# A delta-net inversion by squared 8x8 blocks, decays read as rows, and new cost estimates for the order of the work

## The chip, the core and the metric

The kernel runs on one core of one Trainium2 chip. The metric is the device time of one execution in microseconds (us), median of three runs. TensorE (PE in the profile; PEld is its loading of weights) multiplies matrices, VectorE (DVE) and ScalarE (ACT) do elementwise work, GpSimd (POOL) some more, SyncE (SP) issues most transfers.

## The reference, cut to what matters

One layer: modulated norm, one large input projection, two token mixers side by side (RWKV-7 time mixing and a chunked gated delta net, both in two directions, with 256 context tokens ahead of 256 latent tokens), a gated merge, an output projection, a SwiGLU feed-forward part, a last norm. The change lies in the delta net (8 heads of 128 channels):

```python
gc = jnp.cumsum(chunks(g), axis=-1)
diff = gc[..., :, None] - gc[..., None, :]
decay = jnp.where(incl, jnp.exp(jnp.where(incl, diff, 0.0)), 0.0)
lmat = jnp.where(strict, jnp.einsum('nbhik,nbhjk->nbhij', kb, kc) * decay, 0.0)
rhs = jnp.concatenate([vc * bc[..., None], kb * jnp.exp(gc)[..., None]], axis=-1)
sol = lax.linalg.triangular_solve(lmat, rhs, left_side=True, lower=True, unit_diagonal=True)
...
qk = jnp.where(incl, jnp.einsum('nbhik,nbhjk->nbhij', qc, kc) * decay, 0.0)
q_dec = qc * jnp.exp(gc)[..., None]
k_tail = kc * jnp.exp(gc[..., -1:] - gc)[..., None]
```

`triangular_solve` inverts I + lmat, a unit triangular matrix. The kernel works with chunks of 128 tokens, so with one 128x128 inverse per head, direction and chunk.

## The kernel before

**Stages.** First come the norm and the low-rank projections (`p0`). Then one woven stage holds both mixers and the input projection: the eight RWKV head pairs (`prepare`, `grams`, `inverse`, `values`, `scan`, about 140 to 845 us), then the eight delta-net heads (about 840 to 1385 us), with the weight products for both (`products`) and the rest of the modulation (`ada_rest`, GpSimd transfers and VectorE sums) as filler. After it come the merge products (`pa`, `pb`), `wout` and the feed-forward part.

**The order.** In the woven stage the order on TensorE, VectorE, ScalarE and GpSimd is fixed ahead of time by a planner (`Weave.run`). Each piece of work is a generator that yields operations, waits for PSUM banks (`pab`, two; `pib`, one; `psb`, two; `mmb`, three) or for named events ("gram", h). `Lane` gives each operation a cost, and the planner always takes the operation that can start earliest, then the lower rank. Its costs are never waited for on the chip, where engines wait on semaphores; they only set the order. A list of matmuls is issued in groups of 32; `LAT['turn']` is added where TensorE changes from one kind of product to another. Weights are split into two halves (`whi`, cast by ScalarE; `wlo`, the rest, by VectorE) and multiplied in three passes; the small products of the mixers are float32.

**A delta-net head h.** `features` makes k, v, q (convolution, SiLU, norm); `tokens` transposes k and v and scales k by the decays (`keg`, `kta`); `decays` makes the decay matrix `Ed` of both directions and the decayed queries `Qe`; `head_grams` makes the matrices `LT` and `PT`; `head_inverse` inverts; `head_scan` runs the four chunks with their state. `head_inverse` waits for ("gram", h) and for ("inv", h-1), `decays` for ("gram", h-1), `head_scan` for ("gscan", h-1).

**The inversion (`invert`).** The 128x128 matrix is two 64x64 blocks and their coupling; per head there are 16 blocks of 64 (nu=8 tiles, two halves h). The 16x16 diagonal blocks are inverted by substitution: the blocks are written to DRAM (`scr`), read back with one block per partition (`X`), solved in 15 steps of two VectorE operations, written to DRAM (`tscr`) and read back as `T0` and `Tx`. Then the blocks are doubled to 32 and 64 by small products with evictions between, and to 128 in `head_inverse`, which copies the result into `TF`. The RWKV pairs use the same function with nu=16.

**Decays.** `gm` is a triangular mask times the log decays; a product with `aft` gives the differences, ScalarE exponentiates, GpSimd masks; a product with `ones` gives the running sums for `Qe`.

Of the kernel before, what the change touches and what calls it, by code (L numbers as in the profile page):

```python
# [18 lines left out]
P = 128  # L19
# [10 lines left out]
LAT = dict(dma=2.4, v=1.0, s=1.0, hop=0.5, own=0.13, grp=32, crank=-1, cg=4, turn=0.09)  # L30
# [7 lines left out]
for _name, _w in (("ident", 128), ("ones", 128), ("bd64", 128), ("rmask", 256),  # L38
                  ("qmask", 64), ("tri", 256), ("aft", 256), ("q4", 4), ("q2", 2),
                  ("eps", 1), ("gneps", 1)):  # L40
    _C[_name] = (_n, _n + _w)
    _n += _w
# [12 lines left out]
def const_array():  # L55
# [15 lines left out]
    put("qmask", np.concatenate([(same & (rb % 2 == 1))[:, even], (same & (rb % 2 == 0))[:, ~even]], 1))  # L71
    u = i[:, None]
    v = i[None]
    put("tri", np.concatenate([u <= v, u >= v], 1))
    put("aft", np.concatenate([u > v, u < v], 1))
# [35 lines left out]
class Lane:  # L111
# [5 lines left out]
    def __getattr__(self, name):  # L117

        def op(out, *a, **k):
# [49 lines left out]
class Weave:  # L169
# [55 lines left out]
    def run(self):  # L225
        while self.work:
# [41 lines left out]
def emit(ctx: ExitStack, tc, A, out, dbg=None):  # L268
# [34 lines left out]
    qmask = c_("qmask").rearrange("p (d a c) -> p d a c", d=2, a=2)  # L303
    tri = c_("tri").rearrange("p (d t) -> p d t", d=2)
    aft = c_("aft").rearrange("p (d t) -> p d t", d=2)
# [23 lines left out]
    zero = cst.tile([P, 130], F32, name="zero")  # L329
    G.memset(zero, 0.0)  # L330
# [74 lines left out]
    with tc.tile_pool(name="p0", bufs=1) as p0, \  # L405
# [95 lines left out]
        for part in range(NE + 1):  # L501
# [16 lines left out]
            else:  # L518
                for _ in before:
                    pass  # L520
        for t in tscr:
# [30 lines left out]
    def invert(pool, Lt, parts, nu, which, full, fill):  # L552

# [42 lines left out]
        yield v.transpose(T0[:, us[1]], Tx[:, us[1]])  # L596

# [6 lines left out]

        def half(t, d):
            ax = "p u"[:2 * len(t.shape) - 3]
            return t.rearrange(f"{ax} (a b c) -> {ax} a b c", a=2, b=2)[..., d, :]

        def mm(ps, d, lhs, rhs):
            return [e.matmul(ps[64 * h:64 * h + 64, 32 * i:32 * i + 32], lhs(h, h2 * d + i), rhs(h, h2 * d + i),  # L610
                             start=True, stop=True) for i in range(h2) for h in range(2)]

        Qm = xt[:, :32 * nu].rearrange("p (u c) -> p u c", c=32)
        for d in range(2):
            T0d = half(T0[:, us[d]], d)
            ps = yield pib
            yield mm(ps, d, Lt, lambda h, u: half(N_(h, u), d))
            pv = ps[:, 0:32 * h2].rearrange("p (i a c) -> p i a c", a=2, c=16)
            yield v.tensor_mul(Qm[:, us[d]].rearrange("p i (a c) -> p i a c", a=2), pv,
                               qmask[:, d].unsqueeze(1).to_broadcast([P, h2, 2, 16]))  # L620
            yield mm(ps, d, Nt_, lambda h, u: Qm[64 * h:64 * h + 64, u, :])
            yield v.tensor_add(T0d, pv, T0d)
            weave.release(pib)
            yield v.transpose(Tx[:, us[d]], T0[:, us[d]])
# [19 lines left out]
        qo = pool.tile([P, h2, 32], F32, tag="ivo", name="qo")  # L644
# [6 lines left out]
        if full:  # L651
# [3 lines left out]
            for h in range(2):  # L655
# [8 lines left out]
    abd = dpool.tile([4, 32, P], F32, name="abd")  # L664
    gtok = cst.tile([P, 4, 16], F32, name="gtok")
# [12 lines left out]
               ("ivo", 256, 1), ("iv0", 1024, 1), ("v", 512, 1), ("gt", T, 1))  # L678
# [152 lines left out]
    def grams(p, d):  # L831
# [7 lines left out]
        def four(ops):  # L839
            for o in ops:  # L840
                o.cost *= 0.5
# [199 lines left out]
    def products():  # L1041
# [24 lines left out]
        while todo or nxt:  # L1066
# [27 lines left out]
            else:  # L1094
# [5 lines left out]
    gplaces = (("kvq", 1280, 2), ("l2s", 512, 1), ("gm", 512, 1), ("Ed0", 512, 1), ("Ed1", 512, 1), ("eq", T, 1), ("ob", 8 * T, 1),  # L1100
               ("NW", 1024, 1), ("O", T, 1), ("gy2", T, 1), ("q3", T, 1), ("XT", 512, 1), ("prod", 64, 1))
    shared = dict(kta=("LAl0", 1024, 3), LTg=("LAl1", 1024, 3), keg=("ivx", 1024, 2), iv0=("LAc0", 512, 3), ivx=("LAc0", 512, 3),
                  vt=("LAc1", 512, 3), PT0=("LAc1", 512, 3), PT1=("Pm", 512, 3), Qe=("Pm", 512, 3), Vn=("bon", T, 3), ivo=("bon", T, 3),
# [24 lines left out]
    gs = Shared()  # L1128
    hd = [{} for _ in range(NGH)]
# [6 lines left out]
    def begin():  # L1136
# [6 lines left out]
        t2 = gs.tile([P, 512], F32, tag="gm", name="t2")[:, 0:P]  # L1143
# [12 lines left out]
        for n in (15, 13, 11, 9, 7, 5, 3):  # L1156
# [5 lines left out]
        yield v.tensor_scalar(sp, sp, al, -1.0, ALU.mult, ALU.mult)  # L1162
        ps = yield pab
        yield [e.transpose(ps[:, 0:P], sp, ident), e.transpose(ps[:, P:2 * P], bet, ident)]
# [4 lines left out]
        yield [e.matmul(ps[:, T + 64 * i + 32 * d:T + 64 * i + 32 * d + 32], m[:, d], gtok[:, :, 8 * d:8 * d + 8], start=True, stop=True)  # L1169
               for d in range(2) for i, m in enumerate((tri, aft))] + [e.matmul(ps[:, 3 * P:3 * P + 64], ones, gtok, start=True, stop=True)]  # L1170
        for i, t in enumerate((egc, eta)):
            for d in range(2):
                o = T + 64 * i + 32 * d
                yield s.activation(t[:, :, 8 * d:8 * d + 8], ps[:, o:o + 32].rearrange("p (b c) -> p b c", b=4), AF.Exp)
        yield s.activation(egl, ps[:, 3 * P:3 * P + 64].rearrange("p (b c) -> p b c", b=4), AF.Exp)
# [38 lines left out]
    def features(h):  # L1214
# [5 lines left out]
        if h > 1:  # L1220
            for n in ("tok", "gram"):
# [12 lines left out]
    def tokens(h):  # L1234
# [24 lines left out]
    def decays(h):  # L1259
# [3 lines left out]
        if h:  # L1263
            yield "gram", h - 1
        o["Ed"] = Ed = []
        qe = []
        for d in range(2):
            col = 8 * d + h
            gm = gs.tile([P, 4, P], F32, tag="gm", name="gm")
            yield v.tensor_mul(gm, tri[:, d].unsqueeze(1).to_broadcast([P, 4, P]),  # L1270
                               gtok[:, :, col:col + 1].to_broadcast([P, 4, P]))
            gf = gm.rearrange("p b c -> p (b c)")
            ps = yield pab
            yield e.matmul(ps, aft[:, d], gf, start=True, stop=True)
            ed = gs.tile([P, 4, P], F32, tag=f"Ed{d}", name="Ed")
            yield s.activation(ed.rearrange("p b c -> p (b c)"), ps, AF.Exp)
            weave.release(pab)
            yield g.tensor_mul(ed, ed, tri[:, d].unsqueeze(1).to_broadcast([P, 4, P]))
            Ed.append(ed)
            if d == 0:  # L1280
                yield "feat", h
                yield "scan", NPAIR - 1 if h else NPAIR - 2
                if h > 1:
                    yield "gscan", h - 2
                o["Qe"] = gs.tile([P, 2, T], F32, tag="Qe", name="Qe")
            ps = yield pab
            yield e.matmul(ps[:, :T], ones, gf[:, 0:T], start=True, stop=True)
            eq = gs.tile([P, T], F32, tag="eq", name="eq")
# [410 lines left out]
```

## Time and profile before

| | us |
|---|---|
| median of 3 runs | 2342.38 |
| lowest, highest | 2339.14, 2345.67 |
| profiled execution | 2348.77 |
| its span, first to last instruction | 2346.7 |
| busy: PE, DVE, ACT, POOL | 2223.8, 1557.2, 1047.9, 113.5 |
| granted TensorE clock, mean | 0.975 |

A busy PE is not PE at its peak: matmuls are pipelined and their ends are modelled. L142 is the line of a helper that emits every planned operation, so groups are told apart by their tiles: `mm` are weight products, `pi` those of the inversions, `pa` and `s` other small products. Tiles cut from one large buffer are all named `arena` (`keg`, `kta`, `LT`, `Vn`, `TF`, `Tx`, `T` have names of their own). In a timeline the columns are start, duration, engine, line, operation, and tiles written and read; in a row of grouped lines, count, busy time, mean ns of one, and idle time before with what ended it.

### The profile page before, as it was taken

What the parts mean: (1) busy time and instruction counts of PE and PEld (TensorE: products, weight loads), DVE (VectorE), ACT (ScalarE), POOL (GpSimd) and SP (SyncE); (2) the same over time, 40 slices, a digit from 0 to 9 for tenths busy, and PEclk for the clock granted to TensorE, in tenths of its full rate; (3) what the DMA queues carried; (4) which work ended last, traced back from release to release, by engine and by line L of the source; (5) the groups of instructions that cost most, each with busy time, mean ns of one, the idle gap of its engine ahead of it and who ended that gap; (6) DMA issues with size and microseconds to landing.
All of it is one profiled execution on the core that took longest, in us unless ns stands there. A gap on an engine that the chain in (4) does not pass through costs nothing. (4 is left out here: it accounts for less than half of the span.)

```text
span 2346.7 us, 51488 instructions
## 1 busy us (share of the span) xinstructions
PE 2223.8 (95%) x21368; PEld 1951.7 (83%) x21368; DVE 1557.2 (66%) x3237; ACT 1047.9 (45%) x1863; POOL 113.5 (5%) x183
## 2 busy tenths in 40 slices
PE   7988999999999999999798999999999999999998
PEld 4767677778788777776677989999999999999997
DVE  3447588778986489889878645765666556545454
ACT  3246454544355544344234346544444444444443
POOL 0000000000000011111111003000000000000000
PEclk9999999999999999999789999999999999999999
DMA  9956454434344256657466565663777776566665
GB/s 377 397 148 189 152 134 102 111 83 117 100 109 133 85 172 207 189 167 217 145 191 194 182 219 180 209 214 107 239 233 234 234 238 218 187 185 194 191 191 165
DMA packets 232570, 430.58 MB, mean 183 GB/s; under 512 B 114832, under 2 KB 130064, under 8 KB 227984
## 3 DMA queue, kind: packets, MB, share of 16 engines
q1 hardware_dynamic: 204688, 351.78, 48.4%
q0 software_dynamic: 13824, 50.34, 7.0%
q10 hardware_dynamic: 13824, 25.17, 3.5%
q8 instruction: 167, 2.74, 0.5%
q14 instruction: 67, 0.55, 0.1%
HBM read 401.45 MB, written 25.77 MB: 182 GB/s over the span
## 5 line engine op out<-in xcount | busy, mean ns | idle before, releaser
L357 DVE TENSOR_TENSOR wlo<-wraw,whi 128x1024 fp32r<-128x1024 f32 x328 | 393.5, 1200 | 351.1 <-ACT whi L356 348.2
L356 ACT CAST whi<-wraw 128x1024 fp32r<-128x1024 f32 x328 | 337.7, 1030 | 472.8 <-PE mm L367 413.8
L142 PE MATMUL mm<-hxh,wlo 128*128 128x256 f32 (+1 forms) x1376 | 468.3, 340 | 9.9 <-DVE wlo L142 9.7
L142 PE MATMUL mm<-hxh,whi 128*128 128x256 f32 (+1 forms) x1376 | 469.0, 341 | 3.4 <-ACT whi L142 3.3
L142 PE MATMUL mm<-hxl,whi 128*128 128x256 f32 (+1 forms) x1376 | 468.3, 340 | 0.0
L368 PE MATMUL mm<-hfh,wlo 128*128 128x256 f32 x1344 | 377.1, 281 | 0.4 <-DVE wlo L357 0.4
L366 PE MATMUL mm<-hfh,whi 128*128 128x256 f32 x1344 | 376.5, 280 | 0.0
L367 PE MATMUL mm<-hfl,whi 128*128 128x256 f32 x1344 | 375.2, 279 | 0.0
L142 PEld LDWEIGHTS mm<-hxh,wlo 128*128 128x128 f32 x1376 | 265.6, 193 | 39.4 <-DVE wlo L142 13.0
L142 PEld LDWEIGHTS mm<-hxh,whi 128*128 128x128 f32 x1376 | 265.6, 193 | 31.5 <-issue 6.5
L142 PEld LDWEIGHTS mm<-hxl,whi 128*128 128x128 f32 x1376 | 265.8, 193 | 27.2 <-issue 6.1
L142 DVE TENSOR_TENSOR wlo<-wraw,whi 128x512 fp32r<-128x512 f32 x344 | 236.2, 690 | 62.7 <-ACT whi L142 60.0
L142 ACT CAST whi<-wraw 128x512 fp32r<-128x512 f32 x344 | 205.8, 618 | 112.1 <-PE mm L142 88.9
L366 PEld LDWEIGHTS mm<-hfh,whi 128*128 128x128 f32 x1344 | 253.4, 189 | 0.0
L368 PEld LDWEIGHTS mm<-hfh,wlo 128*128 128x128 f32 x1344 | 252.8, 188 | 0.6 <-DVE wlo L357 0.6
L367 PEld LDWEIGHTS mm<-hfl,whi 128*128 128x128 f32 x1344 | 253.2, 188 | 0.0
L142 DVE TENSOR_TENSOR arena<-arena 128x28 f32<-128x28 f32 (+13 forms) x538 | 132.0, 247 | 32.1 <-DMA arena<-scr 20.4
L366 PE MATMUL mm<-za,whi 128*128 128x256 f32 x512 | 141.8, 277 | 0.0
L367 PE MATMUL mm<-za,whi 128*128 128x256 f32 x512 | 141.7, 277 | 0.0
L368 PE MATMUL mm<-za,wlo 128*128 128x256 f32 x512 | 141.6, 277 | 0.0
L142 DVE SCALAR_TENSOR_TENSOR aw<-aw,ck 128x512 f32<-128x512 f32 x180 | 131.2, 739 | 5.1 <-DMA aw<-ada_rest 4.4
L368 PEld LDWEIGHTS mm<-za,wlo 128*128 128x128 f32 x512 | 96.2, 188 | 0.0
(311 smaller groups left out, 3924.5 us busy)
## 6 DMA issues: line engine op xcount, KB each, us to landing
wraw<-w SPq DMA_DIRECT2D x172, 512.0 KB, 4.3
wraw<-wgu SPq DMA_DIRECT2D x168, 512.0 KB, 4.5
aw<-ada_rest POOLq DMA_DIRECT2D x96, 512.0 KB, 4.7
aw<-ada_first SPq DMA_DIRECT2D x32, 1024.0 KB, 11.5
wraw<-wdn SPq DMA_DIRECT2D x64, 448.0 KB, 3.7
wraw<-wout SPq DMA_DIRECT2D x32, 512.0 KB, 4.7
aw<-ada_gt ACTq DMA_DIRECT2D x64, 256.0 KB, 5.0
wraw<-wdn SPq DMA_DIRECT2D x32, 512.0 KB, 3.6
```

Of the source, the lines that this page charges most:

```text
L142: return Op(self, cost, lambda: getattr(self.engine, name)(out, *a, **k), split)
L356: S.copy(hi[:, c, :M], raw[:, c, :M])
L357: V.tensor_sub(lo[:, c, :M], raw[:, c, :M], hi[:, c, :M].bitcast(F32))
L366: E.matmul(ps, hi, Xh[:, k, :n], start=first and i == 0, stop=False)
L367: E.matmul(ps, hi, Xl[:, k, :n], start=False, stop=False)
L368: E.matmul(ps, lo, Xh[:, k, :n], start=False, stop=last and i == len(wt) - 1)
```

## The change

It changes four things.

- **Inversion of the delta-net heads.** `by_rows` is the old substitution, which the RWKV pairs keep. The heads use `by_squares`: the 8x8 diagonal blocks N are cut out by a mask, and the inverse is (I+N)(I+N^2)(I+N^4), made by products of 64x64x64 in five sets of 16; `double(8)` then takes the blocks to 16. `double` handles both directions in one batch, for the pairs as well.
- **Decays from rows.** `begin` makes running sums with a scan, writes them to DRAM (`cumd`), and `decays` reads them back as rows broadcast to all partitions; the differences are a per-partition add and a minimum with 0 before the exponential. The products with `aft` and `ones` and the masks `gm` go. `Qe` is made in a part of its own, with an event ("Qe", h) that other pieces wait for.
- **Moves.** `keg`, `kta` and `Vn` are scaled by ScalarE instead of VectorE (sixteen operations of 128x128 for four of 128x512; eight for eight).
- **Planner.** New costs for small products and for a change of kind; buffers for `LT` are taken once and kept.

```diff
-LAT = dict(dma=2.4, v=1.0, s=1.0, hop=0.5, own=0.13, grp=32, crank=-1, cg=4, turn=0.09)
+LAT = dict(dma=2.4, v=1.0, s=1.0, hop=0.5, own=0.13, grp=32, crank=-1, cg=4, turn=0.15)
...
-                if rows < 64:
-                    cost = 0.024
-                elif rows == 64:
-                    cost = max(0.066, 0.027 + 0.0008 * n)
-                elif rows < P or m == P:
-                    cost = 0.0054 + 0.00167 * n
-                else:
-                    cost = 0.107
+                tiles = max(1, P // rows) * max(1, P // m) if rows < 96 or m < 96 else 1
+                if tiles > 1:
+                    split = rows, m
+                cost = max(0.033 if tiles < 16 else 0.012, (0.0054 + 0.00167 * n) / min(tiles, 3))
...
-                    start += LAT["turn"]
-                self.split = ops[0].split
+                    start += LAT["turn"] if isinstance(ops[0].split, tuple) or isinstance(self.split, tuple) else 0.02
+                self.split = ops[-1].split
...
+    def by_squares(pool, Lt, parts, nu):
+        a, b, c = (pool.tile([P, nu, 64], F32, tag=t, name=n) for t, n in (("XT", "Dt"), ("iv0", "Dn"), ("ivx", "B")))
...
+        for h in range(2):
+            yield v.tensor_mul(*(t.rearrange("p (d u) c -> p d u c", d=2) for t in (a[hs[h]], parts(h))),
+                               m8[hs[h]].to_broadcast([64, 2, nu // 2, 64]))
+        yield v.transpose(b, a)
+        p1 = yield pib
+        p2 = yield pab
+        yield mm(p1, a, b) + mm(p2, b, a)
+        for h in range(2):
+            yield v.tensor_add(c[hs[h]], b[hs[h]], ident[hs[h], hs[h]].unsqueeze(1).to_broadcast([64, nu, 64]))
+        yield s.copy(flat(E2[:, 0]), p1)
+        weave.release(pib)
+        yield v.tensor_copy(flat(E2[:, 1]), p2)
+        weave.release(pab)
+        p1 = yield pib
+        p2 = yield pab
+        yield mm(p1, E2[:, 1], c) + mm(p2, E2[:, 0], E2[:, 1])
+        yield v.tensor_add(flat(b), p1, flat(c))
+        weave.release(pib)
+        yield s.copy(flat(a), p2)
+        weave.release(pab)
+        p1 = yield pib
+        yield mm(p1, a, b)
+        yield v.tensor_add(flat(c), p1, flat(b))
+        weave.release(pib)
+        yield v.transpose(b, c)
+        yield from double(8, Lt, c, b, flat(a), nu)
+        return c, b, flat(a)
+
+    def double(n, Lt, T0, Tx, xt, nu):
...
+        yield mm(ps, Lt, lambda h, u, d: half(T0[64 * h:64 * h + 64, u, :], d))
+        for d in range(2):
+            yield v.tensor_mul(Qm[:, us[d]].rearrange("p i (a c) -> p i a c", a=na), pv[:, us[d]],
+                               qmask[n == 8][:, d].unsqueeze(1).to_broadcast([P, h2, na, n]))
+        yield mm(ps, lambda h, u: Tx[64 * h:64 * h + 64, u, :], lambda h, u, d: Qm[64 * h:64 * h + 64, u, :])
+        for d in range(2):
+            T0d = half(T0[:, us[d]], d)
+            yield v.tensor_add(T0d, pv[:, us[d]], T0d)
+        weave.release(pib)
+        yield v.transpose(Tx, T0)
...
         def four(ops):
             for o in ops:
-                o.cost *= 0.5
+                o.cost *= 1.0
...
+        yield v.tensor_tensor_scan(t0, ones, sp, 0.0, ALU.mult, ALU.add)
+        yield v.tensor_tensor_scan(t1[:, ::-1], ones, sp[:, ::-1], 0.0, ALU.mult, ALU.add)
+        for d, t in enumerate((t0, t1)):
+            dq(cumd[d], t)
...
-            yield v.tensor_mul(keg[:, d], p4, egc[:, :, col:col + 1].to_broadcast([P, 4, P]))
-            yield v.tensor_mul(kta[:, d], p4, eta[:, :, col:col + 1].to_broadcast([P, 4, P]))
+            for b in range(4):
+                yield s.activation(keg[:, d, b], p4[:, b], AF.Identity, scale=egc[:, b, col:col + 1])
+                yield s.activation(kta[:, d, b], p4[:, b], AF.Identity, scale=eta[:, b, col:col + 1])
...
-            gm = gs.tile([P, 4, P], F32, tag="gm", name="gm")
-            yield v.tensor_mul(gm, tri[:, d].unsqueeze(1).to_broadcast([P, 4, P]),
-                               gtok[:, :, col:col + 1].to_broadcast([P, 4, P]))
-            gf = gm.rearrange("p b c -> p (b c)")
-            ps = yield pab
-            yield e.matmul(ps, aft[:, d], gf, start=True, stop=True)
             ed = gs.tile([P, 4, P], F32, tag=f"Ed{d}", name="Ed")
-            yield s.activation(ed.rearrange("p b c -> p (b c)"), ps, AF.Exp)
-            weave.release(pab)
+            a = cumd[d][0:1]
+            yield dq(ed, bass.AP(a.tensor, a.offset + col * P, [[0, P], [32 * P, 4], [1, P]]))
+            eq = gs.tile([P, T], F32, tag=f"eq{d}", name="eq")
+            yield s.activation(eq, ed[:, 0:2].rearrange("p b c -> p (b c)"), AF.Exp)
+            for b in range(4):
+                yield v.tensor_scalar(ed[:, b], ed[:, b], gtok[:, b, col:col + 1], 0.0, ALU.add, ALU.min)
+            yield s.activation(ed, ed, AF.Exp)
             yield g.tensor_mul(ed, ed, tri[:, d].unsqueeze(1).to_broadcast([P, 4, P]))
...
-            yield e.matmul(ps[:, :T], ones, gf[:, 0:T], start=True, stop=True)
-            eq = gs.tile([P, T], F32, tag="eq", name="eq")
-            yield s.activation(eq, ps[:, :T], AF.Exp)
...
-                yield v.tensor_scalar_mul(Vn[:, d, :], ps[:, P * d:P * d + P], btok[:, bs[d], 8 * d + h:8 * d + h + 1])
+                yield s.activation(Vn[:, d, :], ps[:, P * d:P * d + P], AF.Identity, scale=btok[:, bs[d], 8 * d + h:8 * d + h + 1])
```

More of the change, by code (lines that the diff above doesn't have):

```diff
@@ L550, in unit_rows, with by_rows @@
         return bass.AP(a.tensor, a.offset + (2 * u0 + h) * UNIT, [[64, 64], [2 * UNIT, nu], [1, 64]])
-    def invert(pool, Lt, parts, nu, which, full, fill):
+    def by_rows(pool, parts, nu, which, fill):
         h2 = nu // 2
@@ L598, in N_, with invert @@
+    def invert(pool, Lt, parts, nu, which, full, fill):
+        h2 = nu // 2
+        us = (slice(0, h2), slice(h2, nu))
+        T0, Tx, xt = yield from (by_rows(pool, parts, nu, which, fill) if which is not None else by_squares(pool, Lt, parts, nu))
         def N_(h, u):
@@ L602, in Nt_ @@
             return Tx[64 * h:64 * h + 64, u, :]
[L605 to L624, printed above, removed]
+        yield from double(16, Lt, T0, Tx, xt, nu)
         quads = []
@@ L664, in emit @@
     abd = dpool.tile([4, 32, P], F32, name="abd")
+    cumd = [dpool.tile([P, P], F32, name=f"cumd{d}") for d in range(2)]
     gtok = cst.tile([P, 4, 16], F32, name="gtok")
@@ L1355, in head_scan @@
         yield "tok", h
+        yield "Qe", h
         if h:
```

101 lines of the change are left out of this document (68 added, 33 removed).

## The prediction

> **What bounds the kernel now.** I read the page first, then the time by stage, then when each head's inversion starts and ends, and last the waits of that stretch. The page says TensorE, 95% busy.
>
> ```profile
> span 2346.7 us, 51488 instructions
> PE 2223.8 (95%) x21368; PEld 1951.7 (83%) x21368; DVE 1557.2 (66%) x3237; ACT 1047.9 (45%) x1863; POOL 113.5 (5%) x183
> ```
>
> That is an average over stages, so the busy time by stretch comes next. 400 to 800 us is recurrent time mixing at its steadiest. 837 to 1385 us runs from the first head's inversion to the last head's scan; the two stretches inside it are the first head and the fifth. After 1385 us come only projections and the feed-forward part.
>
> ```profile
> core 0: us, PE busy (x) PEld busy (x) DVE busy (x) ACT busy (x) POOL busy (x), PEclk, DMA share, GB/s
> 400.00:800.00 400.00, 397.07 (x5220) 312.66 (x5220) 312.60 (x778) 194.93 (x483) 11.24 (x30) 1.00 0.40 107
> 837.00:901.00 64.00, 59.73 (x501) 50.02 (x500) 55.94 (x132) 30.06 (x57) 10.81 (x17) 1.00 0.70 214
> 1101.00:1178.00 77.00, 61.31 (x450) 47.77 (x449) 59.78 (x150) 29.59 (x49) 12.12 (x20) 0.81 0.55 166
> 837.00:1385.00 548.00, 497.06 (x4286) 418.61 (x4284) 443.67 (x1108) 225.73 (x427) 70.44 (x110) 0.94 0.62 187
> 1385.00:2347.00 962.00, 931.14 (x7882) 925.53 (x7882) 537.26 (x718) 430.57 (x563) 21.23 (x16) 0.99 0.65 204
> ```
>
> Three things are to be seen. From 400 to 800 us TensorE idles 3 us in 400 at full clock: that stage is bound by its work. In the head stage it idles 548 - 497 = 51 us, at a granted clock of 0.94. The 962 us after it are not touched by the change and are full. So only the head stage has time to give, and the question is what holds it. The first and last rows of the inversions, and the timeline around the fifth head (number 4), tell:
>
> ```profile
> L153 SPq DMA_DIRECT2D scr<-LT x16: 595/596/620, 837.1 to 1306.6; - x16
> ...
> L142 ACT COPY TF<-pi x16: 361/367/372, 897.3 to 1365.7; 64x256 f32<-64x256 f32 x16
> ```
>
> ```profile
> 1086.76 1.12 DVE L142 SCALAR_TENSOR_TENSOR LT<-pa,nbtok,arena 128x128 f32<-128x128 f32 x4
> ...
> 1100.19 0.76 ACT L142 COPY TF<-pi 64x256 f32<-64x256 f32 x2 [1.03 <-PE pi L142]
> ...
> 1102.65 0.42 DVE L142 STREAM_TRANSPOSE T<-LT 64x256 f32<-64x256 f32 x1
> ...
> 1107.38 0.59 SPq L153 DMA_DIRECT2D arena<-scr  x1
> ...
> 1133.93 0.58 SPq L153 DMA_DIRECT2D tscr<-arena  x1
> ...
> 1142.70 0.30 PE L142 MATMUL pi<-T,LT 64*64 64x32 f32 x2
> ...
> 1177.64 0.75 ACT L142 COPY TF<-pi 64x256 f32<-64x256 f32 x2
> ```
>
> Head 4's matrix is complete at 1087.9, but its inversion begins at 1102.7, right behind head 3's last copy at 1101.0: `head_inverse` waits for ("inv", h-1). The eight inversions stand end to end from 837.1 to 1366.0: 529 us, 66 each, all but the whole stage. Inside head 4's, 40 us pass (1102.7 to 1142.7) before the first product: to DRAM, back as rows, thirty small VectorE steps, to DRAM, back. VectorE stands still for two of these trips, 41 us in the stage:
>
> ```profile
> DVE Tx L142 <- DMA T<-tscr: 21.8, 7, 5.9
> ...
> DVE arena L142 <- DMA arena<-scr: 19.2, 7, 7.1
> ```
>
> **The change, part by part.** Per-head prices come from the grouped rows of the head stage (the full transpose's from the whole run):
>
> ```profile
> L142 DVE TENSOR_TENSOR arena<-arena 64x15 f32<-64x15 f32 (+8 forms) x247 | 49.0, 198 | 22.2 <-DMA arena<-scr 19.2
> ...
> L142 DVE TENSOR_SCALAR Vn<-s,btok 128x128 f32<-128x128 f32 x64 | 21.0, 338 | 3.5 <-PE s L142 3.4
> ...
> L142 DVE TENSOR_TENSOR keg<-pa,egc 128x512 f32<-128x512 f32 x14 | 9.5, 678 | 1.3 <-PE pa L142 1.3
> ...
> L142 DVE TENSOR_TENSOR arena<-C,gtok 128x512 f32<-128x512 f32 x14 | 9.4, 673 | 0.1
> ...
> L142 DVE STREAM_TRANSPOSE Tx<-T 128x256 f32<-128x256 f32 x24 | 10.5, 439 | 21.9 <-DMA T<-tscr 21.8
> ...
> L142 DVE STREAM_TRANSPOSE Tx<-arena 128x512 f32<-128x512 f32 x24 | 16.9, 704 | 21.0 <-DMA arena<-tscr 20.8
> ...
> L142 DVE TENSOR_TENSOR arena<-pi,C 128x128 f32<-128x128 f32 x16 | 4.6, 285 | 3.0 <-PE pi L142 2.9
> ...
> L142 ACT CAST whi<-wraw 128x512 fp32r<-128x512 f32 x154 | 91.6, 617 | 72.4 <-PE mm L142 67.3 <-DVE arena L142 2.1 <-DVE aw L142 1.6
> ...
> L142 ACT COPY arena<-s 128x128 f32<-128x128 f32 x16 | 3.6, 265 | 17.5 <-PE s L142 17.3
> ```
>
> *VectorE.* Removed: the substitution, 49.0/8 = 6.1; four 128x512 products for `keg` and `kta`, 2.7; two masks `gm`, 1.35; eight `Vn`, 2.7; four transposes of half size, 1.75. Sum 14.6 us. Added: two masks and two identity sums at 0.68 (the 128x512 row, the nearest), 2.7; one eviction and two sums of that size, 2.0; two full transposes at 0.70, 1.4; in `double(8)` four operations at 0.285 and a transpose, 1.85; eight `tensor_scalar` of 128x128 for the decays, bounded by 0.2 (the small SBUF steps) and 0.34 (`Vn`), taken at 0.285, 2.3. Sum 10.2 us; `double(16)` turns two half transposes into one full one, -0.2. Net -4.6 a head, -37 us in all; and the 41 us of standing still for DRAM go too.
>
> *ScalarE.* Sixteen scalings and eight `Vn` at 0.265, 6.4, and two evictions of 512 columns at 0.62 (the cast of that size): +7.6 a head, +61 us. That is 226 + 61 = 287 of some 530 us, hidden beside TensorE. Were the cover gone, the `whi` casts of the next weights queue behind these 24 operations, and TensorE waits.
>
> *The queues.* SP loses ten transfers a head (of some 0.6 us of issue, as the row of `scr<-LT` shows) and gains two, the decay rows for `Ed0` and `Ed1`. These wait until `head_grams` of the head before has read the buffer; behind them on SP stand the `wraw` loads, covered by three buffers. The rows' trip to DRAM in `begin` is hidden: `begin` copies its scalars at 747.8, and the first `LT` that needs the decays is written at 832.1.
>
> ```profile
> L142 DVE COPY gtok<-pa x1: 225/225/225, 747.8 to 747.8; 128x64 f32<-128x64 f32 x1
> ```
>
> ```profile
> L142 DVE SCALAR_TENSOR_TENSOR LT<-pa,nbtok,arena x64: 308/342/354, 832.1 to 1304.9; 128x128 f32<-128x128 f32 x64
> ```
>
> GpSimd keeps its two mask products a head. I cost these at nothing.
>
> *TensorE.* Added: 80 products of 64x64x64 (16+16, 16+16, 16) and 32 of 64x64x32 in `double(8)`. What such a batch costs among the weights:
>
> ```profile
> 1005.29 0.60 PE L142 MATMUL pa<-arena,C 128*128 128x256 f32 x2
> ...
> 1014.66 1.10 PE L142 MATMUL pa<-arena,C 128*128 128x512 f32 x2 [0.70 <-DVE arena L142]
> ...
> 1347.72 0.28 PE L142 MATMUL mm<-hxh,whi 128*128 128x256 f32 x1
> ...
> 1347.83 0.28 PE L142 MATMUL mm<-hxl,whi 128*128 128x256 f32 x1
> ...
> 1348.04 0.66 PE L142 MATMUL pi<-T,LT 64*64 64x32 f32 x16
> ...
> 1348.62 0.19 PEld L142 LDWEIGHTS mm<-hxh,wlo 128*128 128x128 f32 x1
> ...
> 1363.84 0.68 PE L142 MATMUL pi<-Tx,arena 64*64 64x64 f32 x16
> ```
>
> Sixteen records are eight products (each float32 product has two), and hold TensorE from 1348.04 to 1348.62, 0.58 us; the step into the batch is 0.21 where weights follow at 0.11, so changing kind costs 0.10. 64 columns take as long as 32 (0.68 against 0.66). Added: 14 x 0.58 + 5 x 0.10 = 8.6; two batches fewer in `double(16)`, -0.2. Removed: two float32 products of 512 columns and two of 256, 2 x 1.10 + 2 x 0.60 = 3.4, or 2.9 if a drain of 0.12 is taken from each. Net +5.5 a head, +44 us; the ends are 36 (3.4 removed, no kind changes) and 57 (0.68 a batch).
>
> [...]
>
> *Latency.* From its first product at 1142.7 to its end at 1178.4 head 4 has nine product batches, 4.0 us each with the evictions between. The new inversion replaces 40 us by three VectorE operations (2.1) and five batches (20), and `double(16)` loses two batches (-8): 26 us less, so some 40 instead of 66 a head, 320 us for eight. The chain then no longer fills the stage. What is late next is TensorE: 497 + 44 = 541 us of work.
>
> *The planner's numbers* (small products cheaper, 0.15 for a change of kind) move instructions, not their durations. In the time-mixing stage there are 3 us to win in 400. The 16 merged batches of `invert` save 16 x 0.10 = 2 us; beyond it, a reordering can be worth a per cent of that stage either way, which I take as 0 +- 7.
>
> **Sum.** Of 51 us idle I leave 8 (twice the rate of 400 to 800). A clock of 0.94 means that 0.06 x 548 = 33 us of full-speed time were not granted; with the long waits gone I take 20 of them back. 541 + 8 - 20 = 529 against 548, -19; with the 2 above -21, rounded -22. The profiled execution took 2348.8 us (span 2346.7) and comes to 2327; the median of the runs is 6.4 us lower, so 2342.4 - 22 = **2320**.
>
> [...]
>
> **The rivals.** *All of it comes back.* No idle but 4 us, the full clock, the low end of the added work: 497 + 36 + 4 - 33 = 504, 44 less, 2298. For it: 400 to 800 us does run so. Against: the heads' products wait on evictions far more often.
>
> *TensorE is already the bound.* The added 44 us land on a queue whose idle time comes from other waits (scans, evictions, ScalarE now fuller), so 51 us idle and 0.94 stay: 2342 + 44 - 2 = 2384, and 2363 if a quarter (21) of the 51 + 33 = 84 us of idle and lost clock is won. It decides the sign where less than half of these 84 (42) is won. For it: 497/8 = 62 us of work a head, and 5.5 more, make 67.6, about the head's whole period of 68.5. Against: the inversions stand end to end.
>
> *Nothing comes of it.* The shorter chain pays just for the added products, or the order loses elsewhere what it wins: 2342.
>
> **How the numbers follow.** The forecast 0.56, with its own range 2305 to 2338 (the products' bounds 36 and 57 alone give 2312 to 2333, 10 to 30 us of clock alone 2310 to 2330); all back 0.15; TensorE the bound 0.17; nothing 0.12. 0.3% is 7 us, about what a measurement of this kernel can tell. Faster: 0.56 and 0.15, less a hundredth: 0.70; same 0.12; slower 0.18. The range runs from 2296, the first rival, to 2360, short of the second one's milder case.
>
> **What would show it.** Right: inversions of about 40 us with gaps between them, no VectorE wait on DRAM trips for heads, TensorE busy some 520 us of a head stage of 529, at a clock near 0.98, VectorE about 37 us less, ScalarE about 60 more. Wrong: inversions still end to end, a stage clock still at 0.94, `whi` casts late behind the scalings, or a time-mixing stage that moves by over 7 us.

## The result, and the profile after

The changed kernel takes 2357.14 us (median of 4 runs, 2355.13 to 2360.75) against 2340.98 before: ratio 1.0068, 95% interval 1.0047 to 1.0088. It is 16 us slower; 2320 had been forecast, 22 us faster. The profiled execution took 2356.19 us. Every stretch shown here and below comes from one profiled execution, which can lie 10 us from the median of its kernel (before: 2348.77 against 2340.98), so a few us between two stretches mean little. First the page of the changed kernel, then its busy time by stretch (columns as before):

```profile
span 2354.4 us, 54837 instructions
PE 2247.9 (95%) x23090; PEld 1988.6 (84%) x23090; DVE 1540.0 (65%) x3001; ACT 1108.9 (47%) x2071; POOL 116.8 (5%) x183
```

```profile
400.00:800.00 400.00, 396.20 (x5185) 315.00 (x5184) 316.75 (x793) 197.37 (x485) 14.18 (x31) 1.00 0.41 112
837.00:1385.00 548.00, 520.75 (x6054) 450.92 (x6052) 427.55 (x880) 281.64 (x627) 74.19 (x112) 0.98 0.56 182
837.00:1394.00 557.00, 522.44 (x6066) 452.40 (x6063) 429.87 (x882) 283.40 (x631) 74.19 (x112) 0.98 0.57 184
1394.00:2354.00 960.00, 934.41 (x7880) 929.09 (x7880) 535.78 (x714) 429.71 (x559) 21.29 (x16) 0.99 0.62 203
2093.20:2354.40 261.20, 250.36 (x2118) 249.70 (x2116) 125.88 (x132) 109.41 (x132) 0.00 (x0) 0.99 0.60 180
```

The first merge product starts at 1394.0 (before: 1388.6), so the third row is the whole head stage. To set beside it and beside the last row, two new stretches of the kernel before, cut at the same events:

```profile
837.00:1388.60 551.60, 497.07 (x4287) 418.63 (x4285) 444.11 (x1110) 226.20 (x429) 70.44 (x110) 0.94 0.62 188
2092.50:2346.70 254.20, 242.96 (x2118) 242.31 (x2116) 125.86 (x132) 109.20 (x132) 0.00 (x0) 0.99 0.64 185
```

Two things are to be seen. In the head stage TensorE's busy time is what was forecast, 522 us at a clock of 0.98, but it idles 557 - 522 = 35 us instead of 8. And the last stretch, a piece of the feed-forward part that the change does not touch, takes 261.2 us for the same 2118 matmuls that took 254.2: TensorE is busier by 7.4 us for the same work.

The inversions, by the copies into `TF` and the mask products with which `by_squares` begins (minimum, median and maximum in ns, then first and last start), and those around head 4's end:

```profile
L142 ACT COPY TF<-pi x16: 367/368/370, 886.7 to 1341.9; 64x256 f32<-64x256 f32 x16
...
L142 DVE TENSOR_TENSOR arena<-LT,C x16: 676/689/694, 837.6 to 1298.6; 64x512 f32<-64x512 f32 x16
```

```profile
1100.40 0.68 DVE L142 TENSOR_TENSOR arena<-LT,C 64x512 f32<-64x512 f32 x1
...
1152.25 0.37 ACT L142 COPY TF<-pi 64x256 f32<-64x256 f32 x1
...
1163.43 0.68 DVE L142 TENSOR_TENSOR arena<-LT,C 64x512 f32<-64x512 f32 x1
```

The last inversion ends at 1342.3 instead of 1366.0. Head 4's takes 52 us (the eight take 46 to 57), and 11 us pass before head 5's begins: the inversions no longer stand end to end. The chain is off the path, yet the stage is longer. What ends it, and what is new among ScalarE's waits (us, times, longest):

```profile
1386.41 0.28 PE L142 MATMUL mm<-hxh,wlo 128*128 128x256 f32 x1
1394.01 0.80 PE L363 MATMUL mm<-oah,whi 128*128 128x256 f32 x2 [7.32 <-ACT oah L368]
```

```profile
ACT arena L142 <- DMA arena<-cumd: 33.8, 6, 7.2
```

TensorE does weight products up to 1386.7, 44 us after the last inversion: its own work ends the stage. And ScalarE stands 34 us for decay rows on their way from DRAM.

The last starts of the weight products and of the heads' small products tell how long the chain was beside TensorE's other work, first in the kernel before, then in the changed one:

```profile
L142 PE MATMUL mm<-hxl,whi x1376: 275/282/1415, 135.9 to 1380.7; 128*128 128x256 f32 x126, 128*128 128x512 f32 x71
L142 PE MATMUL s<-arena,C x16: 377/380/635, 935.8 to 1392.2; 128*128 128x256 f32 x16
```

```profile
L142 PE MATMUL mm<-hxl,whi x1376: 274/285/798, 136.4 to 1386.3; 128*128 128x256 f32 x126, 128*128 128x512 f32 x71
L142 PE MATMUL s<-arena,C x16: 377/378/483, 926.8 to 1370.5; 128*128 128x256 f32 x16
```

Before, the weight products ran out at 1380.7 and the last head ended 11.5 us later, beside the first merge products. Now the last head ends 16 us before the weight products do. So the chain outlasted TensorE's other work by some 12 us only, and TensorE was given 44 us of work to shorten it. With rows, then, a head stage that is cut at the first merge product leaves out the end of the last head.

### The profile page after: what moved, and what is told of

Same layout as the page of the kernel before. It is cut to its first block, busy times and chain, and to the rows that moved or that the text cites. A ratio compares the mean times of both kernels' runs of the same rounds, so it can differ in the third digit from the quotient of the medians.

```text
span 2354.4 us, 54837 instructions
## 1 busy us (share of the span) xinstructions
PE 2247.9 (95%) x23090; PEld 1988.6 (84%) x23090; DVE 1540.0 (65%) x3001; ACT 1108.9 (47%) x2071; POOL 116.8 (5%) x183
## 4 chain that ended last, share of the span: by engine, by line
PE 75%; DMA 9%; DVE 8%; issue 4%; ACT 3%; SPq 0%; POOL 0%; DVEq 0%; ACTq 0%; POOLq 0%
PE mm L142 22%; PE mm L365 12%; PE mm L363 12%; PE mm L364 12%; PE s L142 6%; PE pi L142 4%; PE pa L142 4%; DVE arena L142 2%; DMA arena<-cumd 2%; DVE wlo L142 1%; DMA wr<-wgu 1%; PE mm L451 1%; DMA aw<-ada_rest 1%; DVE aw L142 1%; DMA tscr<-arena 1%
## 5 line engine op out<-in xcount | busy, mean ns | idle before, releaser
L142 PE MATMUL mm<-hxl,whi 128*128 128x256 f32 (+1 forms) x1376 | 463.1, 337 | 0.0
L142 ACT ACTIVATE arena<-arena 128x512 f32<-128x512 f32 (+3 forms) x132 | 77.5, 595 | 92.2 <-DVE arena L142 48.6
```

The lines of the kernel that those rows point to most:

```text
L142: return Op(self, cost, lambda: getattr(self.engine, name)(out, *a, **k), split)
```

## The experiments

Where a figure in us is worked out of ratios, it is the difference times 2341. The intervals of the ratios are 0.0013 to 0.0028 (3 to 7 us) to each side.

**1. The same work, 32 bytes further.** The stretch after 2093 us runs the same code in both kernels, but the change shortens the table of constants by 64 columns and moves the tile `zero` (130 columns) out of the same pool, and every buffer behind them lies elsewhere: `whi` began 32 bytes past a multiple of 64 before and begins at a multiple of 64 after. (This is reckoned from the sizes of the tiles; the traces hold no addresses.) So each kernel was run with one tile ahead of the others lengthened, and nothing else changed:

```diff
-    scanm = cst.tile([P, 512], mybir.dt.bfloat16, name="scanm")
+    scanm = cst.tile([P, 528], mybir.dt.bfloat16, name="scanm")[:, 0:512]
```

The changed kernel with it:

> The changed kernel with one small buffer 32 bytes longer, so that everything behind it, the split weights among it, lies 32 bytes further on; no instruction changes its place. In the changed kernel the split weights begin at a multiple of 64 bytes and the moving halves hxh, oah and za at 32 above one; in the kernel before both begin at 32 above one. Theory P (placement: a 256-column weight product steps at 113 ns when both start in the same half of 64 bytes, at 117 when not): steps of hx, oa and za back to 113, some 4900 products times 4 ns, 20 us less than the changed kernel, about 2337 us; hf, mh and zb stay at 117. Rival O (the order of the woven stage costs it all): no change, 2357.

The kernel before with it:

> The kernel before with the same buffer 32 bytes longer. Theory P: hx, oa and za step at 117 ns instead of 113, 20 us more than before, about 2361 us. Rival O: as before, 2341.

The changed kernel with 544, which puts 64 bytes ahead:

> The new kernel with 64 bytes instead of 32 put ahead of its buffers, so that every buffer has its old place within 64 bytes. Theory that the place within 64 bytes sets the step of the weight products: as the new kernel, about 2357, hx, oa and za at 117 to 118 ns. Rival that any shift would have done it (another bound of the memory): about 2343, hx and oa at 114 ns.

Measured: the changed kernel shifted by 32 bytes takes 2342.87 us, ratio to before 1.0003 (0.9985 to 1.002); the kernel before shifted by 32, 2359.57, 1.0070 (1.0049 to 1.0092); the changed kernel shifted by 64, 2363.57, 1.0094 (1.0074 to 1.0115). The stretch of the feed-forward part, first to last, in these three:

```profile
2093.60:2347.60 254.00, 242.98 (x2118) 242.32 (x2117) 125.86 (x132) 109.24 (x132) 0.00 (x0) 0.99 0.63 186
```

```profile
2092.60:2356.10 263.50, 252.30 (x2118) 251.65 (x2116) 125.83 (x132) 109.06 (x132) 0.00 (x0) 0.99 0.61 179
```

```profile
2100.00:2362.40 262.40, 251.31 (x2118) 250.65 (x2116) 125.85 (x132) 109.23 (x132) 0.00 (x0) 0.99 0.61 180
```

2118 matmuls take 243 us at the old place and 250 to 252 at the other, whichever kernel they are in. The place is worth 15 us in the changed kernel (1.0068 against 1.0003) and 16 in the one before. At equal place the change is worth nothing that these runs can tell (0.9985 to 1.002).

Two runs sought the rule by lengthening `arena` (9544 columns to 9552), beside the 32 bytes in the changed kernel and alone in the one before, so that all large buffers lie alike within 64 bytes:

> The changed kernel with the 32 bytes of the first run and the large buffer 32 bytes longer as well, so that hf, mh and zb also start in the same half of 64 bytes as the weights. Theory P: every 256-column product at 113 ns; against the first run 5600 products times 4 ns, 22 us less, about 2315 us. Rival O: 2357; a rival in which only the weights' own start matters: like the first run, 2337.

> The kernel before with only the large buffer 32 bytes longer: weights and all moving halves start in the same half of 64 bytes. Theory P: hf, mh and zb at 113 ns, 22 us less than before, about 2319 us. Against the third run it then gives the worth of the change by itself, with equal placement: within 5 us of it if the head stage's idle time was only traded for the added products. Rival O: 2341.

They took 2352.46 (1.0037, 1.0020 to 1.0054) and 2355.66 (1.0050, 1.0031 to 1.0069), both slower than without, where the theory had 2315 and 2319; in the second the feed-forward stretch went from 254 to 261 us though its weights had not moved. So neither the place of the weights alone decides, nor that weights and moving halves lie alike; which buffers must stand how stays open. All further versions of the changed kernel carry the 32 bytes, so that their weights lie as before the change.

**2. Is the stage TensorE's?** The eighty squaring products of a head, each issued twice:

```diff
-                    for u in range(nu) for h in range(2)]
+                    for u in range(nu) for h in range(2) for _ in range(2)]
```

> The shifted changed kernel with each of the 80 squaring products of a head issued twice in a row. By the batch row that is 80 times 72 ns, 5.8 us a head, 46 in all. If TensorE's work sets the head stage (T, and what is left under W): 30 to 46 us more, 2373 to 2389. If the stage is still set by a chain of waits with TensorE idle beside it: under 15 us more.

2393.73 us, 1.0224 (1.0198 to 1.0251), 52 us more than without, a little above the 30 to 46 expected; the profiled executions differ by 34. Its head stage, to the first merge product:

```profile
837.00:1431.00 594.00, 553.12 (x7268) 482.69 (x7264) 427.16 (x872) 282.68 (x624) 74.71 (x112) 0.99 0.54 173
```

The same stretch of the shifted new kernel without the doubling:

```profile
837.00:1396.80 559.80, 520.02 (x6074) 449.23 (x6074) 431.17 (x885) 284.16 (x636) 73.63 (x112) 0.98 0.59 183
```

Idle is 41 us in the one and 40 in the other: with squares the stage grows by what TensorE is given, here 33 us of busy time for 1280 more records. A batch twice as long also lengthens each inversion, so the growth alone would not tell TensorE's work from the chain. The end of the stage does: the last copy into `TF` starts at 1377.8 (in the changed kernel at 1341.9), and weight products go on to 1422.8.

```profile
L142 PE MATMUL mm<-hxl,whi x1376: 276/281/797, 135.5 to 1422.8; 128*128 128x256 f32 x126, 128*128 128x512 f32 x71
```

**3. Each part undone.** In the shifted new kernel, one part at a time: the planner's old numbers (f2), the old decays by `aft` and `ones` (f5), the inversion by rows (f3), and `keg`, `kta` and `Vn` on VectorE (f6). The cores of the last two edits (f6 turns back `Vn` in the same way):

```diff
-    ... lambda hh: LT[64 * hh:64 * hh + 64, :, 64 * hh:64 * hh + 64], 8, None, True, v)
+    ... lambda hh, d: [(0, LT[64 * hh:64 * hh + 64, 4 * d:4 * d + 4, 64 * hh:64 * hh + 64])], 8, h % 2, True, v)
```

```diff
-            for b in range(4):
-                yield s.activation(keg[:, d, b], p4[:, b], AF.Identity, scale=egc[:, b, col:col + 1])
-                yield s.activation(kta[:, d, b], p4[:, b], AF.Identity, scale=eta[:, b, col:col + 1])
+            yield v.tensor_mul(keg[:, d], p4, egc[:, :, col:col + 1].to_broadcast([P, 4, P]))
+            yield v.tensor_mul(kta[:, d], p4, eta[:, :, col:col + 1].to_broadcast([P, 4, P]))
```

> The shifted changed kernel with the planner's numbers of before (costs of products, 0.09 for every change of kind, the halved costs in the grams). Theory W: the numbers only move instructions, within 7 us of 2343. Rival E (the new estimates are the fault: 37 ns planned for a product that takes 72): 10 to 20 us faster, 2325 to 2333.

> The shifted changed kernel with the decays of before (masks and products, no rows from DRAM), the rest of the change kept. The products cost 2.9 us a head on TensorE, 23 in all. Theory W: the wait of 35 us goes, some 20 us are won and 23 paid, 2343 to 2348. Rival T: 23 paid, 2366.

> The shifted new kernel (2342.9 in its own comparison) with the heads' inversion by rows again, all else as in it: decay rows, moves, new planner numbers. Theory that the 80 squaring products cost about what they hold TensorE and that their shorter chain wins no more than a part of it: faster than the shifted new kernel by 10 to 25 us, so about 2325, ratio to before near 0.993; the inversions end to end again at 60 us or more each, TensorE busy some 470 to 485 us in the head stage. Rival that the shorter chain pays for its products: the long chain ends the stage again, 2350 to 2360, ratio 1.004 to 1.008.

> The shifted new kernel with keg, kta and Vn scaled by VectorE again. Theory that TensorE's own work ends the head stage: no engine beside it decides, within 5 us of the shifted new kernel (2343), ScalarE some 50 us less busy in the stage and VectorE some 40 more. Rival that the fuller ScalarE holds up the casts of the weights: about 10 us faster. Rival that VectorE is next to the bound: 10 us or more slower.

And two more: the planner told that decay rows land 7 us later than it reckons (f1; no instruction added, only the order), and the kernel before with the new planner numbers alone (p1):

```diff
-            yield dq(ed, bass.AP(a.tensor, a.offset + col * P, [[0, P], [32 * P, 4], [1, P]]))
+            yield dq(ed, bass.AP(a.tensor, a.offset + col * P, [[0, P], [32 * P, 4], [1, P]])) + 7.0
```

> The shifted changed kernel (first run) with one number of the planner changed: it takes the decay rows to arrive 7 us later than it reckoned, about the 10 us that they take in the trace. Theory W (the wait moved: with equal placement the change is worth nothing because ScalarE, which takes its work in order, now stands still for the decay rows, 35 us in the head stage, as VectorE did for the inversion's trips before): TensorE's idle time in the head stage falls by about 20 us, 2325 us. Rival T (TensorE is the bound, its idle time lies elsewhere): 2343.

> The kernel before with the new planner numbers alone. Theory that these numbers are worth about 15 us wherever they are used (undoing them in the shifted new kernel cost that): 2327, ratio 0.9935, the gain in the head stage. Rival that they only pay with the squaring products, which they price right: within 4 us of before, 2338 to 2346.

| kernel | us | ratio to before |
|---|---|---|
| new, shifted (e1) | 2342.87 | 1.0003 |
| old planner numbers (f2) | 2353.64 | 1.0068 |
| old decays (f5) | 2346.34 | 1.0026 |
| inversion by rows (f3) | 2350.70 | 1.0036 |
| moves undone (f6) | 2341.22 | 1.0000 |
| rows planned late (f1) | 2338.15 | 0.9991 |
| before, new planner numbers (p1) | 2333.19 | 0.9966 |

To undo the planner numbers alone costs 15 us, squares 8, decay rows 5, the moves nothing; the 8 is little more than the intervals allow, the 5 is not clear of them. The first three look like gains; but the kernel that has them all equals the one before. Each part was measured with the others in place, and they are not independent. f5 and f6 came as their first expectation had it. f2 met neither: the new numbers, suspected of harm, help. f1 lies between its two: ScalarE's wait went (below), but 5 us were won where the theory of the moved wait had about 20. For f3 the rival came, the long chain that ends the stage (last copy into `TF` at 1381.7), with TensorE busy only 474 us of it; p1 lies between its two expectations.

**4. The parts put together one by one.** All at the same place, all with new planner numbers and merged batches: rows with old decays and old moves (g1), squares with both old (g2), rows with decay rows (g4); squares with decay rows is f6. g3 has late rows and moves undone together.

> The shifted new kernel with inversion by rows, old decays and old moves: of the change, the planner numbers and the merged batches of the doubling (pairs and heads) are left. Theory that the merged batches cost nothing and that decay rows and moves are what the long chain pays for: as the kernel before with the new planner numbers alone, 2333 (ratio 0.9966). Rival that the merged batches, which keep each half waiting for both, lengthen the chain: 2345 to 2350.

> The same with the inversion by squares: squares, planner numbers and merged batches, with old decays and old moves. Theory that TensorE's own work ends the stage with squares (512 products of weights less or more do not matter, only what is added to TensorE): between 2342 and 2350, that is 10 to 15 above the kernel with rows and the planner numbers, since the old decays give TensorE back 23 us of work. Rival that squares are better than rows at any setting by the 8 us seen before: 2325.

> The shifted new kernel with inversion by rows and old moves, decay rows kept. Theory that the decay rows, planned too early, hold up ScalarE and with it the long chain: between 2343 and 2350, near the kernel with moves (2350.7). Rival that the moves to ScalarE are what the long chain pays for: 2330 to 2335, the decay rows saving TensorE 23 us that the stage has no use for.

> The shifted new kernel with the decay rows planned 7 us later and the moves undone. If the late rows are worth the 5 us seen, and the moves nothing: 2337. Rival that the two cure the same thing, ScalarE's queue: 2341, as with the moves undone alone.

| | inversion by rows | by squares |
|---|---|---|
| old decays | 0.9949 (g1, 2331.79 us) | 1.0004 (g2, 2345.46) |
| decay rows | 1.0056 (g4, 2355.96) | 1.0000 (f6, 2341.22) |

(g3: 2338.87, 0.9992, between its two expectations.) g1 and g2 came as the theory had them; g4 lies above both of its cases. From g1, squares cost 13 us, decay rows 25, and both together 12. With decay rows in place squares look like a gain of 13; with squares in place decay rows look like nothing lost. Head stages, to the first merge product, of g1, g2, g4 and f6 in this order:

```profile
837.00:1382.20 545.20, 491.06 (x4309) 417.24 (x4307) 446.32 (x1109) 224.69 (x429) 72.42 (x111) 0.94 0.63 191
```

```profile
837.00:1390.70 553.70, 528.45 (x6106) 455.16 (x6104) 460.14 (x935) 236.17 (x449) 72.08 (x111) 0.98 0.55 178
```

```profile
837.00:1394.70 557.70, 483.47 (x4215) 411.20 (x4213) 448.56 (x1133) 224.72 (x428) 75.28 (x111) 0.92 0.63 193
```

```profile
837.00:1389.40 552.40, 517.91 (x6027) 446.71 (x6025) 461.40 (x968) 233.90 (x448) 72.99 (x112) 0.98 0.59 185
```

Idle is length less busy: 54, 25, 74, 34 us. Squares (first to second row) take 29 us of idle away and add 37 us of busy time, and the stage is 8 us longer. Decay rows take TensorE work away (491 to 483, 528 to 518) and put back idle time: 20 us with rows, 9 with squares. With rows the chain is on the path, and they lengthen it (and what lies behind the first merge product, at 1394.7 in g4, is not even counted: the last small product of its heads starts at 1415.8, in g1 at 1391.5). The last copies into `TF` of g1 and g4:

```profile
L143 ACT COPY TF<-pi x16: 365/368/370, 911.8 to 1362.6; 64x256 f32<-64x256 f32 x16
```

```profile
L142 ACT COPY TF<-pi x16: 365/367/369, 903.1 to 1386.7; 64x256 f32<-64x256 f32 x16
```

**5. Why decay rows lengthen the chain.** ScalarE waits 48.5 us for them in g4's head stage, with the chain's copies queued behind, and VectorE, which solves the chain's 30 small steps a head, waits 22.7 us for the ScalarE operations on the rows (in g1, without rows, 1.6 us):

```profile
ACT arena L142 <- DMA arena<-cumd: 48.5, 7, 12.3
```

```profile
DVE arena L142 <- ACT arena L142: 22.7, 7, 4.1
```

So g5 is g4 with the line of f1, the rows planned later:

> The kernel with inversion by rows and decay rows (moves undone; 2356.0, ratio 1.0056), with the planner told that the decay rows land 7 us later. Theory that ScalarE's early wait for the rows (48.5 us in its head stage) holds up the copies of the long chain behind it: the wait falls under 10 us, the inversions end some 20 us earlier, and the time comes to 2332 to 2338, near the 2331.8 with old decays. Rival that the late rows themselves make the decay matrices late for the chain, whatever is planned: 2350 or more, with the matrices LT complete after the head before has been inverted.

My theory fell. The wait is gone from ScalarE's list, as expected, but the time is 2375.06, 1.0143 (1.0115 to 1.0170), 20 us over g4, and the last copy into `TF` comes at 1411.2. Nor did the rival's sign come: head 7's matrix is on its way to `scr` at 1312.6, before head 6 is inverted at 1336.8. VectorE now waits for filler loads (us, times, longest), where g1 had 1.9 us of it and g4 7.6:

```profile
DVE aw L142 <- DMA aw<-ada_rest: 38.4, 7, 9.8
```

```profile
DVE aw L143 <- DMA aw<-ada_rest: 1.9, 3, 0.8
```

And the trips to DRAM are slower. DMA issues of the head stage, g1 and then g5 (count, KB each, median us to landing):

```profile
scr<-T SPq DMA_DIRECT2D x16, 64.0 KB, 3.9
T<-tscr SPq DMA_DIRECT2D x16, 64.0 KB, 2.8
```

```profile
wraw<-w SPq DMA_DIRECT2D x74, 512.0 KB, 5.3
arena<-cumd SPq DMA_DIRECT2D x14, 256.0 KB, 9.7
...
scr<-T SPq DMA_DIRECT2D x16, 64.0 KB, 6.0
T<-tscr SPq DMA_DIRECT2D x14, 64.0 KB, 4.9
```

In g4 these two trips took 5.5 and 2.6 us. That the decay rows' own transfers get in the way of the chain's trips and of the filler's loads fits most of these rows; it is argued, not shown. Shown is that planning the rows later is no cure under rows: it takes away the waits on the rows and brings others. What makes g4 slow stays open. With squares, which make no trips, the same line took ScalarE's wait from 35 us (e1, then f1) to 5, and the ratio from 1.0003 to 0.9991, though these intervals overlap:

```profile
ACT arena L142 <- DMA arena<-cumd: 35.1, 6, 7.7
```

```profile
ACT arena L142 <- DMA arena<-cumd: 4.6, 3, 2.3
```

**A version that beats both** is g1: the kernel before with new planner numbers and merged batches. 2331.79 us, 0.9949 (0.9930 to 0.9968), 12 us under the kernel before, 28 under the changed one. Of it the planner numbers alone give 8 (p1); the 4 us between p1 and g1 lie within the intervals.

## Why the prediction was wrong

**TensorE's term was right as a sum.** Forecast: 497 + 44 - 20 = 521 us busy; measured 522 at the forecast clock. Its two halves were each too large. Old decays' products, priced at 23 us, are worth 11 us of busy time at an equal clock (g2 to f6). No run shows the drain of 0.12 us a product that makes 2.9 a head of 3.4. In the kernel before, the next product starts 0.25 us after two records of 256 columns (1005.29) and 0.54 after two of 512 (1014.66); by these steps my estimate is 1.6 a head, 13 us for eight:

```profile
1005.54 0.58 PE L142 MATMUL mm<-hxl,whi 128*128 128x512 f32 x1
...
1015.20 0.80 PE L142 MATMUL mm<-hxh,whi 128*128 128x512 f32 x1
```

Squares, at 8.6 us a head 69, added 37 from g1 to g2 while the clock rose from 0.94 to 0.98, which is worth some 22 (0.04 x 545): by this estimate 59 in all. And a batch issued twice held TensorE for less than the price: 33 us for eighty products a head, where 0.58 for eight gives 46.

**The step that failed is "of 51 us idle I leave 8".** The stage keeps 35 (in the same borders it had 54.5). With 35 in place of 8 the forecast sum, 541 + 8 - 20 = 529, becomes 556, and the stage measures 557. I took the end-to-end inversions as the cause of nearly all idle time. They were the cause of some 29 us of it (g1 to g2). Of what stays, the longest waits are for the output of the RWKV mixer, which is read back when the last weight product has ended, for state updates and for `Vn`:

```profile
PE mm L363 <- ACT oah L368: 7.3, 1, 7.3
PE s L142 <- DVE St L142: 6.1, 5, 2.7
PE s L142 <- ACT Vn L142: 5.2, 3, 2.4
```

The chain itself went as told: no VectorE wait for the heads' DRAM trips, ends 24 us earlier, gaps between inversions. But one inversion takes about 52 us, not 40. Fillers stand between its VectorE steps (in head 4 a modulation sum at 1101.0 between the two mask products); that they make up the 12 us is not shown.

**"I cost these at nothing", of the queues,** was the second failure. Decay rows of 256 KB land in 9.4 us (median), and with them the stage has 9 us more idle time with squares and 20 with rows. With squares this costs nothing in the end (g2 against f6). The cover I named (the trip in `begin`, three weight buffers) was for the write and for SP, not for ScalarE, which stood 33.8 us for the rows.

**The mechanism that came was the rival "TensorE is already the bound"**, which I gave 0.17. Its deciding point was 42 us won of idle and lost clock. Won were 20 of idle (54.5 to 34.6) and 22 of clock (0.06 x 552 = 33 to 0.02 x 557 = 11), together 42, and the stage came out near it: 551.6 to 557 us. That the measured 2357 lies near this rival's milder 2363 is luck, for 15 us of it are the place of the buffers. At equal place the number is that of "Nothing comes of it" (0.12), but the shorter chain does not pay for its products (squares cost 13 us from g1); the planner numbers make up for it. The for-argument of "TensorE is already the bound", 62 + 5.5 us of work a head against a period of 68.5, was the better reading.

**The place of the buffers was in no rival.** It makes the difference between nothing (1.0003) and 1.0068. The prediction has no term for it, and the profile before could not show it; the diff of the kernels did show that a table and a tile ahead of the buffers change.

**The planner's 0 +- 7** was too narrow: 8 us in the kernel before (0.9953 to 0.9979), 15 in the new one. It was reckoned for the time-mixing stage alone, and in the changed kernel that stage ends where it did (the first inversion starts at 837.6 instead of 837.1). It hid a loss of the same size: the rest of the change costs 13 us (g1 to e1).

**VectorE and ScalarE.** VectorE lost 14 us in the stage, not 37, though the masks came as priced (689 ns against 680). About 10 of the missing 23 us are overlap: the busy times of the single groups, which count overlapping operations twice, fell by 24 (504 to 481). Another 2.9 is a misread row: the 49.0 us of the substitution mix nine forms, and the one of 128x256 is not part of it. The rest is not settled; with the moves undone the time is the same (f6), so it is off the path. ScalarE gained 57 of 61. Its scalings are 0.37 to 0.41 us long, not the 0.265 of a plain copy, but in a run of them one starts 0.25 us after the other, so the price held. From the groups of the head stage, and from its timeline:

```profile
L142 ACT ACTIVATE kta<-pa,eta 128x128 f32<-128x128 f32 x58 | 23.8, 410 | 0.0
...
L142 ACT ACTIVATE Vn<-s,btok 128x128 f32<-128x128 f32 x64 | 22.2, 372 | 31.5 <-PE s L142 31.5
```

```profile
1090.45 0.37 ACT L142 ACTIVATE keg<-pa,egc 128x128 f32<-128x128 f32 x1
1090.71 0.36 ACT L142 ACTIVATE kta<-pa,eta 128x128 f32<-128x128 f32 x1
1090.96 0.37 ACT L142 ACTIVATE keg<-pa,egc 128x128 f32<-128x128 f32 x1
```

**The clock** in the stage came to 0.98, and 22 of 33 us returned, as forecast (20). Of the other 11, 10 lie at TensorE's waits: 20 us of the stage passed at a clock of 0.50, at or just behind four waits of 3.05, 2.42, 2.58 and 2.70 us, which end at 973.7, 1046.0, 1109.3 and 1175.0. The first of these waits, and the four stretches:

```profile
973.66 1.12 PE L142 MATMUL pi<-Dn,arena 64*64 64x64 f32 x16 [3.05 <-DVE Dn L142]
```

```profile
972.10:978.80 6.70, 5.14 (x70) 4.93 (x71) 5.22 (x9) 0.00 (x0) 1.06 (x2) 0.50 0.38 80
1047.20:1050.60 3.40, 3.40 (x10) 2.65 (x9) 3.37 (x8) 0.64 (x2) 0.42 (x2) 0.50 0.94 356
1108.70:1115.40 6.70, 6.14 (x17) 5.08 (x18) 6.52 (x15) 2.17 (x5) 1.71 (x3) 0.50 0.66 222
1177.00:1180.20 3.20, 3.20 (x40) 2.43 (x40) 2.87 (x4) 1.65 (x4) 2.19 (x2) 0.50 0.50 159
```

## What to carry to other kernels

When a chain stands end to end on an engine's timeline, that shows that the chain has no slack, not that the rest has: add up the other engine's work for the period first, and look which of the two ends last and by how much (here 12 us of 552, 2%); if they are that close, pay no TensorE time for a shorter chain. Judge the parts of a change by adding them one at a time to the old kernel; taking them one at a time from the new one made two losses look like gains here. And before any of it, give both kernels the same buffer addresses (15 to 16 us here).

## What the hardware showed that was not expected

- The same 2118 matmuls of 256 columns and their loads took 243 us or 250 to 252 us, depending on 32 bytes in the place of their buffers; which buffers it is stays open. Over the whole kernel this was 15 to 16 us, 0.7%.
- In the changed kernel's head stage 256 KB of rows broadcast to all partitions landed in 9.4 us (median; 9.7 to 10.5 in f1, g4 and g5), where 512 KB of weights took 4.7 (4.4 to 5.3).
- Scalings of a 128x128 block with a factor per partition on ScalarE are 0.37 to 0.41 us long, but start 0.25 us apart in a run: the length of one record is not its price.
- In the head stage of the changed kernel the granted clock was 0.50 for 3 to 7 us at or just behind four waits of TensorE of 2.42 to 3.05 us.
